# Two layers in fp32 pairs: a longer attention pipeline, low parts moved to POOL, a weight cast placed earlier, two plain up pages

## The chip, the cores and the metric

The kernel runs on one core of one Trainium2 chip. The metric is the device time of one execution in microseconds. Three runs of the kernel before took 2409.1, 2407.9 and 2407.92; their median is 2407.92.

## The reference

A block of 1024 tokens and 1024 features goes through two layers, all in float32. The first is a hybrid layer:

```python
h = rms_norm(x, norm_g)
u = jnp.einsum('bsd,dc->bsc', h, w_in)
v_c, b_c, c_c, z_c, q, k, v, z_a, gate_logits = jnp.split(u, SPLIT_POINTS, axis=-1)
y_c = b_c * causal_depthwise_conv(c_c * v_c, conv_w) * silu(z_c)
y_a = y_c @ w_conv_out
q, k = rms_norm(q), rms_norm(k)                       # 16 query heads, 4 key heads, 64 wide
o = sliding_window_attention(q, k, v, sinks) * silu(z_a)   # window 128, blocks of 128
y_b = o @ w_attn_out
g_a, g_b = split(sigmoid(gate_logits + gate_b))
x = x + (g_a * y_a + g_b * y_b) @ w_out
```

The second layer adds a mixer of pooled features and gated linear attention, a cross attention over 256 memory rows, and a feed-forward part: `u = h @ w_up` (2 x 2816 columns), a causal convolution of width three over each column of `u`, then `(silu(gate) * val) @ w_down`. A final rms norm ends it.

## The kernel before

**Number format.** Every large matrix product is done with float32 values cut in two: a high part (a cast to fp32r, on ScalarE) and a low part (value minus high part, one subtraction). A product is three matmuls, high by high, high by low, low by high. In the code names end in `h` and `l`, or `hi` and `lo`. Activations are kept transposed, feature by token, as tiles of 128 features by 512 tokens, in two halves `h`.

**Weights.** Weights arrive as pages of 128 x 1024 (512 KB): all of an output block's 1024 input rows. `Weights` walks a fixed list (`_stream`). `load` starts a DMA on SP into one of two raw buffers `wr`; `pf` casts the high part `wh` on ScalarE (two buffers) and puts the low part on a list `late`; `flush` (line 342) does the listed subtractions on VectorE, into `wl` (two buffers). `get` hands out a page and prefetches the next one. With `spare=True` the two parts go to other tiles, `wsh` and `wsl`.

**Plain and Strassen products.** A plain page is two calls of `dense` (line 381), one a half, each of 8 x 3 = 24 matmuls of 512 columns. Where two pages share an activation, `wino` (line 400) does both with seven products of 4 x 3 matmuls (a Winograd form of Strassen's scheme). It needs sums of the four quarters of the activation, T1 to T4, and of the two pages, S1 to S4. `sums` (line 448) makes the T on VectorE, with casts on ScalarE; `make` (line 290) makes the S on POOL (lines 298 to 306), with casts on ScalarE and low parts on VectorE (lines 302, 314, 330), one step a tick.

**Order of work.** All engines execute in the order in which the program is written; nothing reorders it. Side work is written as Python generators on the list `side`. `tick` flushes the low parts, moves `make` one step and moves every generator one step. `dense` ticks once in its middle and its caller once behind it, so that a plain page has four ticks. Tiles of PSUM: three banks `mm`, two `s`, two `t`, one `o`.

**The z pages.** At the start x goes through the norm in two halves. `first_two` runs the pages z0 and z1 on half 0, then both on half 1, whose tiles a side thread is still making; another side thread, `hT_sums`, makes T1 to T4 beside it, with quarters that it reloads from DRAM (`ht`, `hraw`). The third page is cast where `first_two` calls `W.pf()`, behind the product of z0 on half 1. Then come z2, z3 and the first pairs in `wino`.

**Attention.** While the pages `co` (conv output) and then `ao` (attention output) are multiplied, 16 halves each, the side generator `attention` (line 1160) runs 32 units, each of 4 heads over a block of 128 queries. In step i it does: the exponentials of unit i-1 on ScalarE (`expo`); the product with V of unit i-4 (`values`) into the single bank `o`, multiplied by VectorE into the head tiles (line 1155); for every second unit the difference of two blocks of V on POOL (`differ`); the scaling of unit i-1's probabilities by one over their sum on POOL (`finish`, line 1108); the transposes of unit i-2 on TensorE with their cut into high and low, and masked copies of both on POOL (`turn`, lines 1128 to 1138); the scores of unit i (`scores`, line 1078), copied by ScalarE and masked by VectorE, with row maxima. When a group of heads is done for a half, the four head tiles are cut one a step (`split`, low part on VectorE, line 377). At the start of half 1 of `co` the program waits for conv rows that another side thread (`reload`) is still bringing, with ticks that have no matmuls of their own.

**The up projection.** 22 pairs of pages (gate `fg`, value `fv`). The first FF_STD = 3 pairs run plain, the first in `first_two`, beside the norm of half 1 and the T sums; the rest run in `wino`. Behind each product stand its copy, three taps of the convolution (ScalarE, then two on VectorE, lines 1767 and 1768) and the gating (line 1775).

Of the kernel before, what the change touches and what calls it, by code (L numbers as in the profile page):

```python
# [11 lines left out]
ALU = mybir.AluOpType  # L12
# [8 lines left out]
DFF = 2816  # L21
NFF = DFF // P
FF_GROUPS = ((0, 6), (6, 12), (12, 18), (18, 22))
FF_STD = 3
POOL_WINDOWS = (2, 4, 8, 16)


# [51 lines left out]
def _stream():  # L79
    st = [("v", 0), ("v", 1)]  # L80
    st += [("z", 0, j) for j in range(4)]
    st += [("pair", ("z", 1, j), ("z", 1, j + 1)) for j in (0, 2)]
    st += [("pair", ("q", p, j), ("q", p, j + 1)) for p in range(2) for j in (0, 2)]
    st += [("pair", ("gb", m), ("gb", m + 1)) for m in range(0, KT, 2)]
    for c in range(KT):
        st += [("pair", ("cc", c), ("cv", c)), ("pair", ("cz", c), ("cb", c))]
    st += [("pair", ("ga", m), ("ga", m + 1)) for m in range(0, KT, 2)]
    st += [("co", m) for m in range(KT)] * 2
    st += [("ao", m) for m in range(KT)] * 2
    st += [("wo", m) for m in range(KT)] * 2  # L90
    st += [("p2", 0)]
    for p in range(2):
        st += [("q2", p), ("k2", p), ("v2", p, 0), ("v2", p, 1)]
    st += [("r2", 0), ("r2", 1), ("p2", 1), ("p2", 2), ("r2", 2), ("p2", 3), ("r2", 3)]
    st += [("wo2", m) for m in range(KT)] * 2
    for m in range(KT):
        st += [("xq", m), ("mk", m), ("mv", m // 4, m % 4)]
    st += [("xq", m) for m in range(KT)]
    st += [("xo", m) for m in range(KT)] * 2
    for f in range(NFF):  # L100
        st += [("fg", f), ("fv", f)] if f < FF_STD else [("pair", ("fg", f), ("fv", f))]
    for g in range(len(FF_GROUPS)):
        st += [("fd", g, m) for m in range(KT)]
    return st
# [12 lines left out]
def _body(es, tc, nc, wp, vec, xT, memT, gk2, pw, cst, out, dbg):  # L117
# [9 lines left out]
    V, S, G, T = nc.vector, nc.scalar, nc.gpsimd, nc.tensor  # L127
# [6 lines left out]
    def hp(s, dt=F32, shape=(P, HT)):  # L134
        return hpool.tile(list(shape), dt, name=nm(s), tag="hp")

    def tp(s, dt=F32, shape=(P, HT)):
        return tpool.tile(list(shape), dt, name=nm(s), tag="tp")
# [25 lines left out]
    def ps(tag, shape=(P, HT)):  # L164
        return psum.tile(list(shape), F32, name=nm("ps" + tag), tag=tag,
                         bufs={"mm": 3, "s": 2, "t": 2, "o": 1}[tag])

    def f(ap):
        return ap.bitcast(F32)
# [8 lines left out]
    def tick():  # L178
        W.flush()
        W.step()  # L180
        for g in list(side):
            if next(g, StopIteration) is StopIteration:
                side.remove(g)
# [23 lines left out]
    class Page:  # L207
        def __init__(self, his, los):
            self.his, self.los, self.n = his, los, 1024 // len(his)
# [19 lines left out]
    class Weights:  # L229
        def __init__(self):  # L230
            self.names = _stream()
            self.raw, self.cut = {}, {}
            self.late = []
            self.gen = None
            self.nd = self.ns = self.ng = self.out = 0
            self.limit = -1

        def load(self, name):
            n = ncols(name)
            raw = wpool.tile([P, 1024], F32, name=nm("wr"), tag="wr")  # L240
            nc.sync.dma_start(raw[:, :n], wp[PAGE[name], :, :n])
            self.out += 1
            return raw
# [98 lines left out]
        def flush(self):  # L342

            for lo, raw, hi in self.late:
                V.tensor_tensor(lo, raw, f(hi), ALU.subtract)  # L345
            self.late = []

        def get(self, name, pf=True, deep=False):
# [17 lines left out]
    W = Weights()  # L366
# [7 lines left out]
    def split(src, s, lo_in=None, eng=V):  # L374
        hi, lo = hp(s + "h", F32R), (lo_in or hp)(s + "l", F32R)
        S.copy(hi, src)
        eng.tensor_tensor(lo, src, f(hi), ALU.subtract)
        return hi, lo

    def mm3(out_ap, lh, ll, rh, rl, first, last):  # L380
        T.matmul(out_ap, lh, rh, start=first, stop=False)  # L381
        T.matmul(out_ap, lh, rl, start=False, stop=False)  # L382
        T.matmul(out_ap, ll, rh, start=False, stop=last)  # L383

    def dense(w, act, h, n=HT, msz=P, mid=None):

        o = ps("mm", (P, n))
        k = len(act)
        for kt in range(k):
            ah, al = act[kt][h]  # L390
            mm3(o[:msz], *w(kt * msz, msz), ah, al, kt == 0, kt == k - 1)
            if kt == k // 2 - 1:
                tick()
                if mid is not None:
                    mid()
        return o
# [115 lines left out]
            evac(dense(w, act, h), h)  # L512
            tick()

    def first_two(na, nb, act, ea, eb, spare=False):

        a = W.get(na)
        ea(dense(a, act, 0), 0)
        tick()
        b = W.get(nb, pf=False)  # L520
        eb(dense(b, act, 0), 0)
        tick()
        while None in [x[1] for x in act]:
            tick()
        if spare:
            W.pf(spare=True)
        o = dense(a, act, 1)
        if not spare:
            W.pf()
        ea(o, 1)  # L530
        tick()
        eb(dense(b, act, 1), 1)
        tick()
# [101 lines left out]
    def grid(n):  # L635
        return [[None, None] for _ in range(n)]
# [31 lines left out]
    hR, hT = grid(KT), grid(KT)  # L668
# [191 lines left out]
    def z_out(p, j, h, o):  # L860
        t = tp("z")
        S.activation(t, o, AF.Silu)
        zd[p, j, h] = dram("zd")
        nc.sync.dma_start(zd[p, j, h], t)
# [44 lines left out]
        wino((na, nb), X, lambda x: evac(0, 0, x), c22, c12, lambda y: evac(1, 0, y))  # L909

    side.append(hT_sums())
    first_two(("z", 0, 0), ("z", 0, 1), hT, *[lambda o, h, j=j: z_out(0, j, h, o) for j in range(2)])
    for j in (2, 3):
        both(("z", 0, j), hT, lambda o, h: z_out(0, j, h, o))
    while "T1" not in XB:
# [103 lines left out]
    qT, oT = {}, [[[None, None] for _ in range(4)] for _ in range(2)]  # L1019
# [137 lines left out]
    osp = grid(KT)  # L1157

    def attention():
        units = [Unit(p, h, b, half) for h in range(2) for p in range(2) for b in range(4) for half in range(2)]  # L1160
        n = len(units)
        todo = []
        dv = None
        for _ in range(5):
            yield
        for i in range(n + 4):
            if 0 <= i - 1 < n:
                units[i - 1].expo()
            if 0 <= i - 4 < n:
                units[i - 4].values(dv)  # L1170
                if i % 8 == 3:
                    u = units[i - 4]
                    todo += [(u.p, j, u.h) for j in range(4)]
            if i % 2 and 0 <= i - 3 < n and units[i - 3].n:
                dv = units[i - 3].differ()
            if 0 <= i - 1 < n:
                units[i - 1].finish()
            if 0 <= i - 2 < n:
                units[i - 2].turn()
            if i < n:  # L1180
                units[i].scores()
            if i in (8, 16):
                side.append(att_in(i // 16, 1))
            if todo:
                p, j, h = todo.pop(0)
                osp[4 * p + j][h] = split(oT[p][j][h], "o")
            yield
        while todo:
            p, j, h = todo.pop(0)
            osp[4 * p + j][h] = split(oT[p][j][h], "o")  # L1190
            yield
# [21 lines left out]
    while None in [yc[c][0] for c in range(KT)]:  # L1213
        tick()
    side.append(attention())
    for h in range(2):
        for m in range(KT):
            w = W.get(("co", m))
            gate_in(gin, gad, m + 1, h)
            if h == 0 and m == 3:  # L1220
                side.append(reload([(ycd[c][1], yc[c], 1) for c in range(KT)], "yc", 1, 1))
            while None in [yc[c][h] for c in range(KT)]:
                tick()
            o = dense(w, yc, h)
            t = gin[m, h]
            V.tensor_tensor(t, t, o, ALU.mult)
            mcd[m][h] = dram("mcd")
            nc.sync.dma_start(mcd[m][h], t)
            tick()
# [3 lines left out]
    def ao_in(m, h):  # L1233
        gate_in(gbi, gbd, m, h)
        gate_in(cin, mcd, m, h)

    xs = grid(KT)
    ao_in(0, 0)
    for h in range(2):
        for m in range(KT):  # L1240
# [7 lines left out]
            o = dense(w, osp, h)  # L1248
# [146 lines left out]
    o = glow_dense(1)  # L1395
# [136 lines left out]
    act = [cat[i] for i in order]  # L1532
# [301 lines left out]
    first_two(("fg", 0), ("fv", 0), xn, up0.plain(0), up0.plain(1), True)  # L1834
    for ft in range(1, FF_STD):
        up = Up(ft)
# [6 lines left out]
    fill_banks(XF["B11"][0][0])  # L1843
    for ft in range(FF_STD, NFF):
        if ft == NFF - 1:
# [26 lines left out]
    act = group(0, 0)  # L1872
# [5 lines left out]
    for g in range(1, 3):  # L1878
        act = group(g)
# [25 lines left out]
    act = group(3)  # L1905
    for h, c in ((0, slice(0, HT)), (1, slice(0, 256)), (1, slice(256, HT))):
        n = c.stop - c.start
        last = c.start > 0
        nrm, sqs = Norm(), []
        for m in range(KT):  # L1910
# [6 lines left out]
            o = dense(pages[m], [[None] * h + [(x[h][0][:, c], x[h][1][:, c])] for x in act], h, n)  # L1917
# [145 lines left out]
```

## Time and profile before

| | |
|---|---|
| profiled execution | 2407.34 us, of which the span of the trace 2405.6 |
| TensorE (PE) busy | 2366.1 us, 98%, 11574 matmuls |
| VectorE (DVE) busy | 1487.5 us, 62%, 2317 instructions |
| ScalarE (ACT) busy | 1009.5 us, 42%, 1869 |
| POOL busy | 577.8 us, 24%, 554 |
| DMA | 264.97 MB, mean 110 GB/s |

A row of the timeline gives start and duration in us, the engine, the line of the kernel, the operation, the tile written and those read, the shapes, and in brackets the idle time of that engine before it with what ended it. TensorE's instructions are pipelined: a duration is longer than the distance to the next start, so the distance between two starts is the rate.

### The profile page before, as it was taken

What the parts mean: (1) busy time and instruction counts of PE and PEld (TensorE: products, weight loads), DVE (VectorE), ACT (ScalarE), POOL (GpSimd) and SP (SyncE); (2) the same over time, 40 slices, a digit from 0 to 9 for tenths busy, and PEclk for the clock granted to TensorE, in tenths of its full rate; (3) what the DMA queues carried; (4) which work ended last, traced back from release to release, by engine and by line L of the source; (5) the groups of instructions that cost most, each with busy time, mean ns of one, the idle gap of its engine ahead of it and who ended that gap; (6) DMA issues with size and microseconds to landing.
All of it is one profiled execution on the core that took longest, in us unless ns stands there. A gap on an engine that the chain in (4) does not pass through costs nothing.

```text
span 2405.6 us, 30929 instructions
## 1 busy us (share of the span) xinstructions
PE 2366.1 (98%) x11574; PEld 1952.4 (81%) x11574; DVE 1487.5 (62%) x2317; ACT 1009.5 (42%) x1869; POOL 577.8 (24%) x554
## 2 busy tenths in 40 slices
PE   8999999999999999999999999999999999999998
PEld 8788888888887787887888888888888888888887
DVE  7744346666537997555445556455798888873435
ACT  5444433333346664334322334443555555552112
POOL 3235433333303552121001120001233333310003
PEclk9999999999999999999999999999999999999999
DMA  4533322122247534621100245322422222245222
GB/s 166 181 126 135 124 84 71 62 70 70 84 170 260 184 135 150 210 90 50 39 28 29 88 127 179 97 83 91 160 88 79 79 84 79 93 139 167 84 78 93
DMA packets 107510, 264.97 MB, mean 110 GB/s; under 512 B 12096, under 2 KB 14560, under 8 KB 107360
## 3 DMA queue, kind: packets, MB, share of 16 engines
q1 hardware_dynamic: 104880, 256.70, 31.3%
q0 software_dynamic: 1936, 5.77, 0.7%
q8 instruction: 91, 1.49, 0.2%
q10 hardware_dynamic: 544, 0.52, 0.1%
q14 instruction: 59, 0.48, 0.1%
HBM read 203.18 MB, written 59.77 MB: 109 GB/s over the span
## 4 chain that ended last, share of the span: by engine, by line
PE 88%; DVE 6%; ACT 3%; DMA 1%; issue 1%; POOL 0%; SPq 0%; DVEq 0%; POOLq 0%; ACTq 0%
PE psmm L381 14%; PE psmm L383 13%; PE psmm L382 13%; PE pss L410 6%; PE pss L412 5%; PE pss L411 5%; PE psmm L410 4%; PE psmm L412 4%; PE psmm L411 4%; PE pst L410 2%; PE pst L412 2%; PE pst L411 2%; PE pso L410 2%; PE pso L412 2%; PE pso L411 2%
## 5 line engine op out<-in xcount | busy, mean ns | idle before, releaser
L345 DVE TENSOR_TENSOR wl<-wr,wh 128x1024 fp32r<-128x1024 f32 (+1 forms) x147 | 180.3, 1226 | 97.7 <-ACT wh L281 97.5
L410 PE MATMUL pss<-T,wsh 128*128 128x512 f32 x588 | 232.0, 395 | 0.1
L412 PE MATMUL pss<-T,wsl 128*128 128x512 f32 x588 | 230.1, 391 | 0.0
L411 PE MATMUL pss<-T,wsh 128*128 128x512 f32 x588 | 229.4, 390 | 0.0
L330 DVE TENSOR_TENSOR wsl<-ws,wsh 128x512 fp32r<-128x512 f32 x196 | 208.3, 1103 | 33.4 <-ACT wsh L312 32.4
L564 POOL TENSOR_TENSOR sq<-sq,sq 128x512 f32<-128x512 f32 (+1 forms) x58 | 70.9, 1222 | 608.7 <-ACT sq L560 605.1
L281 ACT CAST wh<-wr 128x1024 fp32r<-128x1024 f32 (+1 forms) x147 | 148.2, 1008 | 149.7 <-PE psmm L382 128.5
L298 POOL TENSOR_TENSOR ws<-wr 128x512 f32<-128x512 f32 x49 | 69.8, 1425 | 567.5 <-DMA wr<-in_wp_dram 459.0
L381 PE MATMUL psmm<-xnh,wh 128*128 128x512 f32 x448 | 179.3, 400 | 5.0 <-ACT wh L281 5.0
L383 PE MATMUL psmm<-xnh,wl 128*128 128x512 f32 x448 | 175.9, 393 | 0.7 <-DVE wl L345 0.7
L382 PE MATMUL psmm<-xnl,wh 128*128 128x512 f32 x448 | 175.5, 392 | 0.0
L410 PE MATMUL psmm<-xnh,wh 128*128 128x512 f32 x392 | 153.9, 393 | 0.0
L412 PE MATMUL psmm<-xnh,wl 128*128 128x512 f32 x392 | 153.2, 391 | 0.0
L411 PE MATMUL psmm<-xnl,wh 128*128 128x512 f32 x392 | 152.6, 389 | 0.0
L410 PEld LDWEIGHTS pss<-T,wsh 128*128 128x128 f32 x588 | 110.4, 188 | 25.6 <-DVE cb L990 2.4
L412 PEld LDWEIGHTS pss<-T,wsl 128*128 128x128 f32 x588 | 110.3, 188 | 25.2
L411 PEld LDWEIGHTS pss<-T,wsh 128*128 128x128 f32 x588 | 110.4, 188 | 23.6
L383 PE MATMUL psmm<-fh,wl 128*128 128x512 f32 (+1 forms) x300 | 116.0, 387 | 1.1 <-DVE wl L345 1.1
L560 ACT ACTIVATE sq<-x 128x512 f32<-128x512 f32 (+1 forms) x80 | 47.1, 588 | 164.7 <-DVE x L1267 110.4
L381 PE MATMUL psmm<-fh,wh 128*128 128x512 f32 (+1 forms) x300 | 115.9, 386 | 0.0
L382 PE MATMUL psmm<-fl,wh 128*128 128x512 f32 (+1 forms) x300 | 115.9, 386 | 0.0
L302 DVE TENSOR_TENSOR wl<-wr,wh 128x1024 fp32r<-128x1024 f32 x49 | 66.0, 1346 | 70.8 <-ACT wh L296 70.8
(453 smaller groups left out, 6231.7 us busy)
## 6 DMA issues: line engine op xcount, KB each, us to landing
wr<-in_wp_dram SPq DMA_DIRECT2D x238, 512.0 KB, 3.7
act<-fa SPq DMA_DIRECT2D x44, 256.0 KB, 2.1
fr<-act SPq DMA_DIRECT2D x44, 256.0 KB, 4.4
wr<-in_wp_dram SPq DMA_DIRECT2D x24, 384.0 KB, 3.1
xd<-x SPq DMA_DIRECT2D x32, 256.0 KB, 4.4
x<-xd SPq DMA_DIRECT2D x32, 256.0 KB, 4.0
x<-in_xT_dram SPq DMA_DIRECT2D x16, 256.0 KB, 5.2
zd<-z SPq DMA_DIRECT2D x16, 256.0 KB, 2.0
```

Source lines behind the costliest of these rows:

```text
L281: S.copy(hi[:, :n], raw[:, :n])
L298: G.tensor_tensor(sg[0], a21, a22, ALU.add)
L302: V.tensor_tensor(l12, r1, f(h12), ALU.subtract)
L330: V.tensor_tensor(lo, raw, f(hi), ALU.subtract)
L345: V.tensor_tensor(lo, raw, f(hi), ALU.subtract)
L381: T.matmul(out_ap, lh, rh, start=first, stop=False)
L382: T.matmul(out_ap, lh, rl, start=False, stop=False)
L383: T.matmul(out_ap, ll, rh, start=False, stop=last)
L410: T.matmul(o, lh, rh, start=first and kt == 0, stop=False, skip_group_check=True)
L411: T.matmul(o, lh, rl, start=False, stop=False, skip_group_check=True)
L412: T.matmul(o, ll, rh, start=False, stop=kt == 3, skip_group_check=True)
L564: eng.tensor_tensor(self.acc, self.acc, sq, ALU.add)
```

## The change

Five edits. (1) In `attention` the step does the transposes of unit i-3 instead of i-2, the product of unit i-5 instead of i-4, and the difference of V for that unit, one step later each; the loop has 37 steps instead of 36. (2) The low part of a finished head tile is done on POOL inside that loop (those left over behind it stay on VectorE). (3) From the start of the attention to the end of the `co` pages, `flush` does the weights' low parts on POOL. (4) For the z pages `first_two` prefetches the third page right behind fetching the second, ahead of the second's product on half 0. (5) FF_STD is 2: the third up pair runs in `wino`.

```diff
-FF_STD = 3
+FF_STD = 2
...
             for lo, raw, hi in self.late:
-                V.tensor_tensor(lo, raw, f(hi), ALU.subtract)
+                self.eng.tensor_tensor(lo, raw, f(hi), ALU.subtract)
...
-    def first_two(na, nb, act, ea, eb, spare=False):
+    def first_two(na, nb, act, ea, eb, spare=False, ahead=False):
...
         b = W.get(nb, pf=False)
+        if ahead:
+            W.pf()
         eb(dense(b, act, 0), 0)
...
         o = dense(a, act, 1)
-        if not spare:
+        if not spare and not ahead:
             W.pf()
...
-        for i in range(n + 4):
+        for i in range(n + 5):
             if 0 <= i - 1 < n:
                 units[i - 1].expo()
-            if 0 <= i - 4 < n:
-                units[i - 4].values(dv)
-                if i % 8 == 3:
-                    u = units[i - 4]
+            if 0 <= i - 5 < n:
+                units[i - 5].values(dv)
+                if i % 8 == 4:
+                    u = units[i - 5]
                     todo += [(u.p, j, u.h) for j in range(4)]
-            if i % 2 and 0 <= i - 3 < n and units[i - 3].n:
-                dv = units[i - 3].differ()
+            if i % 2 == 0 and 0 <= i - 4 < n and units[i - 4].n:
+                dv = units[i - 4].differ()
             if 0 <= i - 1 < n:
                 units[i - 1].finish()
-            if 0 <= i - 2 < n:
-                units[i - 2].turn()
+            if 0 <= i - 3 < n:
+                units[i - 3].turn()
...
-                osp[4 * p + j][h] = split(oT[p][j][h], "o")
+                osp[4 * p + j][h] = split(oT[p][j][h], "o", eng=G)
...
     side.append(attention())
+    W.eng = G
     for h in range(2):
         for m in range(KT):
             w = W.get(("co", m))
...
     xs = grid(KT)
+    W.eng = V
     ao_in(0, 0)
```

## Rows read from the trace of the kernel before

**Rows 1.** The chain that ended last, its shares of the span by engine.
```profile
PE 88%; DVE 6%; ACT 3%; DMA 1%; issue 1%; POOL 0%; SPq 0%; DVEq 0%; POOLq 0%; ACTq 0%
```

**Rows 2.** Waits of TensorE, whole span: total us, times, longest us.
```profile
PE pso L1151 <- DVE o L1155: 6.7, 7, 1.9
...
PE pst L1128 <- POOL pr L1108: 2.3, 3, 1.2
```

**Rows 3.** Windows: length; busy us (instructions) of PE, PEld, DVE, ACT, POOL; clock; DMA.
```profile
722.00:760.00 38.00, 35.71 (x216) 27.32 (x214) 26.07 (x68) 21.14 (x65) 10.19 (x13) 1.00 0.85 318
760.00:800.00 40.00, 34.82 (x188) 26.44 (x187) 37.63 (x104) 28.21 (x93) 16.01 (x24) 0.87 0.56 192
800.00:870.00 70.00, 70.00 (x419) 56.31 (x418) 64.29 (x177) 47.54 (x162) 41.08 (x62) 1.00 0.48 164
870.00:930.00 60.00, 55.61 (x300) 43.27 (x299) 50.69 (x132) 35.15 (x113) 31.75 (x47) 0.97 0.27 93
...
92.36:99.17 6.81, 5.22 (x11) 3.64 (x12) 2.92 (x4) 4.96 (x8) 0.00 (x0) 0.50 0.55 185
```

**Rows 4.** Timeline of the z pages: ScalarE, TensorE and VectorE between 80 and 120 us.
```profile
81.67 0.60 ACT L862 ACTIVATE z<-psmm 128x512 f32<-128x512 f32 x1
92.81 1.04 ACT L281 CAST wh<-wr 128x1024 fp32r<-128x1024 f32 x1
...
93.91 0.79 PE L381 MATMUL psmm<-xnh,wh 128*128 128x512 f32 x1 [4.96 <-ACT wh L281]
119.58 0.39 PE L412 MATMUL psmm<-xnh,wl 128*128 128x512 f32 x1
...
100.02 0.69 DVE L482 TENSOR_TENSOR ht<-ht,x 128x512 f32<-128x512 f32 x1 [4.30 <-DMA ht<-hraw]
102.43 1.22 DVE L345 TENSOR_TENSOR wl<-wr,wh 128x1024 fp32r<-128x1024 f32 x1
115.84 1.21 DVE L302 TENSOR_TENSOR wl<-wr,wh 128x1024 fp32r<-128x1024 f32 x1
```

**Rows 5.** Groups of VectorE, 800 to 870: busy us, mean ns, idle before.
```profile
L345 DVE TENSOR_TENSOR wl<-wr,wh 128x1024 fp32r<-128x1024 f32 x5 | 7.4, 1484 | 0.0
L377 DVE TENSOR_TENSOR ol<-o,oh 128x512 fp32r<-128x512 f32 x7 | 5.9, 840 | 0.0
```

**Rows 6.** Groups of POOL, whole span: busy us, mean ns, idle before.
```profile
L305 POOL TENSOR_TENSOR ws<-wr,wr 128x512 f32<-128x512 f32 x49 | 82.2, 1677 | 0.0
...
L564 POOL TENSOR_TENSOR sq<-sq,sq 128x512 f32<-128x512 f32 (+1 forms) x58 | 70.9, 1222 | 608.7 <-ACT sq L560 605.1 <-issue 2.6 <-DVE sq L564 0.9
```

**Rows 7.** Timeline of TensorE: products of values at a bare tick, and steady.
```profile
787.30 0.47 PE L1151 MATMUL pso<-pch,vh 128*128 128x512 f32 x1 [2.54 <-ACT pr L1100]
...
805.88 0.40 PE L1151 MATMUL pso<-pch,vh 128*128 128x512 f32 x1
806.12 0.39 PE L1151 MATMUL pso<-pch,vl 128*128 128x512 f32 x1
...
811.56 0.40 PE L1151 MATMUL pso<-pch,vh 128*128 128x512 f32 x1
```

**Rows 8.** Timeline of ScalarE: the first exponential of two successive bare ticks.
```profile
785.08 0.20 ACT L1095 ACTIVATE sd<-sd 128x4 f32<-128x4 f32 x1 [3.25 <-DVE sd L1091]
...
790.42 0.20 ACT L1095 ACTIVATE sd<-sd 128x4 f32<-128x4 f32 x1 [0.76 <-DVE sd L1091]
```

**Rows 9.** Windows of the up stage, columns as in rows 3.
```profile
1753.90:1761.20 7.30, 7.30 (x34) 6.05 (x33) 6.90 (x13) 6.33 (x10) 0.00 (x0) 1.00 0.10 36
1773.80:1781.20 7.40, 7.40 (x34) 6.11 (x34) 7.03 (x6) 4.83 (x8) 7.27 (x4) 1.00 0.00 0
```

**Rows 10.** Timeline of the up stage: VectorE, SP's queue, TensorE's first fill matmuls.
```profile
1758.83 1.23 DVE L345 TENSOR_TENSOR wl<-wr,wh 128x1024 fp32r<-128x1024 f32 x1 [0.37 <-ACT wh L281]
...
1750.09 0.33 SPq L241 DMA_DIRECT2D wr<-in_wp_dram  x1
...
1783.59 0.62 PE L444 MATMUL pss<-xnh 128*128 128x512 f32 x2
```

More of the change, by code (lines that the diff above doesn't have):

```diff
@@ L236, in __init__ @@
             self.limit = -1
+            self.eng = V
         def load(self, name):
@@ L911, in _body @@
     side.append(hT_sums())
-    first_two(("z", 0, 0), ("z", 0, 1), hT, *[lambda o, h, j=j: z_out(0, j, h, o) for j in range(2)])
+    first_two(("z", 0, 0), ("z", 0, 1), hT, *[lambda o, h, j=j: z_out(0, j, h, o) for j in range(2)], ahead=True)
     for j in (2, 3):
```

## The prediction

> **What bounds the kernel now.** I began with the chain that ended last: 88% of the span runs over TensorE [rows 1]. It executes nearly the same matmuls after the change, so the question is where it stands still, and what takes over once it doesn't. The list of who waited for whom has VectorE's product out of the one-buffer PSUM tile `pso` as the longest wait, and POOL's scaling of the probabilities as a short one [rows 2]. The windows put both into the attention [rows 3]: TensorE is idle 2.3 us of 722–760, 5.2 of 760–800, none of 800–870, 4.4 of 870–930, together 11.9. After the longer stalls the granted clock falls to half (1.2 GHz): the mean of 0.87 in 760–800 and 0.97 in 870–930 is 0.13 x 40 + 0.03 x 60 = 7.0 us of lost clock, in part idle anyway. So the attention loses between 11.9 and 18.9 us; I take 17. VectorE is busy 37.6 of 40 us there and 64.3 of 70: it is what TensorE waits for.
>
> The second loss is at 89 us. TensorE stands for 5.0 us in front of the third z page, waiting for ScalarE's cast [rows 4], and then runs 6.8 us at half clock [rows 3], another 3.4: some 8 us. The up stage loses nothing: its windows have no idle time on TensorE, though VectorE is busy 6.9 of 7.3 us [rows 9].
>
> **Attention.** A steady tick, from one product of values to the next, is 5.68 us [rows 7]; a 512-column matmul takes 0.23 [rows 7], so the 12 of the dense half are 2.7 and the attention's own part is 3.0. Per tick VectorE has 64.3 x 5.68 / 70 = 5.2 us, POOL 41.1 x 5.68 / 70 = 3.3 [rows 3].
>
> The two moved kinds of work are 7.4 and 5.9 us of those 70 [rows 5], 1.1 us a tick: VectorE falls to 4.1. On POOL a 128x512 two-input operation has a mean of 1.22 us, or 1.68 for the group that meets most of VectorE's traffic [rows 6]. A page of weights has twice the columns and comes every second tick, so it adds 1.22 to 1.68 a tick; 13 of the 16 finished-head splits lie inside the loop of 37 steps, 0.43 to 0.59 a tick. POOL goes to 5.0, at most 5.6, of 5.68. I take the lower price, because the two-input SBUF operations that collide with POOL here are the very ones that leave VectorE; the row for the weights shows the collision now, 1.48 us against 1.23 elsewhere [rows 5, 10].
>
> The longer pipeline moves the transposes one tick later and the product of values one tick later. POOL's scaling then has 5.68 us more before TensorE asks for it; its waits (2.3 us) go [rows 2]. Behind a low part that POOL does late stands POOL's own queue (the differences of V, the scaling, the two masked copies), and TensorE is next to ask: for the differences one tick on, for the rest two. Finished low parts of weights are needed about a tick and a half after they are queued. Lags below some 5.7 us cost nothing.
>
> What stays: two ticks of the loop in `co` run without a dense half, since they only wait for the reloaded conv rows; at the first of them TensorE stands idle for 2.5 us [rows 7]. ScalarE and VectorE hand a loop to each other (exponentials, high part, score copies, masking, maximum, next exponentials) that takes 790.42 − 785.08 = 5.34 us [rows 8], and no part of the change shortens it. Two such ticks can cost 2 x (5.34 − 3.0) = 4.7; TensorE is now one product ahead, so I take 2.5. In the first `ao` pages the merge's cast stands in front of the exponentials on ScalarE and the low parts are back on VectorE: 1.5 left there. New loss 4, old 17: the attention gives **−13 us** (bounds: −17, and 0 if POOL's queue takes over).
>
> The Trainium skill (GPSIMD Engine Reference, Engine selection) speaks against this part: elementwise work with two inputs belongs on VectorE, POOL being about twice as slow. The trace agrees on the ratio (1.22 us for 512 columns against 1.23 for 1024). By that rule the move would be a loss; it is the fourth case below.
>
> **The cast ahead.** The z cast stood at 92.81 on ScalarE, behind a row of casts for the Strassen sums, which wait for VectorE [rows 4]. It now stands right behind the first z activation (81.67), done by about 84, its low part on VectorE by about 86; the wait at 88.9 is gone. It delays what stood between by 1.0 and 1.2 us, the same that is removed later. TensorE goes on at 88.8, needs the next page at about 100.1, and there it stops again: that page's low part runs at 102.43, because VectorE stands in order behind a sum whose input lands at 100.02 [rows 4]. That load is issued behind z's store, which moves by little. So TensorE waits from 100.5 to 103.8. It ends the page near 114.5 and meets the first pair's low part, 115.84 + 1.21 = 117.05, after the same chain of loads. Its third matmul stood at 119.58 [rows 4]; it can stand at 117.3, or at 118.9 if the clock falls again. Of 8 us lost, 2.3 or 0.7 come back: I take **−1.8** (bounds −8, 0).
>
> **Two plain up pages.** The third up pair was 8 x 12 = 96 matmuls and becomes 84: 12 x 0.23 = −2.7. Its price lies in VectorE's queue. The pair begins on TensorE at 1783.59 − 96 x 0.23 = 1761.5 [rows 10]. In the kernel before, the low part used there ran at 1758.83 and ended 1.4 us ahead of use [rows 10], though it is queued 36 matmuls ahead of it, at 1753.2: VectorE was over 5 us behind. Now the pair's first low part stands a tick later in that queue, behind two more sums and two conv taps (2.9 us); without more it would end near 1762.9, just in time. But POOL forms the pair's four weight sums as soon as the second page lands, about 3.8 us after 1750.09, in that very stretch. VectorE did 13 instructions in 7.30 us with POOL idle, and 6 in 7.40 us beside four such sums [rows 9]: some 3.5 us of its work are lost. The low part ends near 1766.2 against a use at 1762.7 (three fill matmuls and two others stand ahead): 3.5 us of wait, and 1.3 more for the low part of the pair's first sum. That is 4.8 − 2.7 = +2.1, and a little for the clock: **+2.5** (bounds −2.7 without a stall; +6 with one stretch of half clock as long as the one at 92 us).
>
> The Trainium skill (SBUF — State Buffer, SBUF: two separate sides) says that VectorE with two SBUF inputs and GpSimd lock one port pair against each other for whole instructions; the trace agrees, the 13 against 6 being its price.
>
> The attention's tiles don't hold the longer pipeline back: a score tile takes the buffer of a masked copy whose last product stands earlier in the same step, on TensorE ahead of the scores. The moved low parts free their raw buffers later by POOL's 1.2 us, against loads with a page of lead.
>
> **Sum.** −13 − 1.8 + 2.5 = −12.3. The profiled execution took 2407.3 (span 2405.6), so 2395.0; the median of the runs is 0.6 above it: **2395.6**.
>
> **Rivals.** *The up stage does not stall.* If VectorE catches up during the second plain page, the up stage gives −2.7: 2407.9 − 13 − 1.8 − 2.7 = 2390.4. For it: without POOL's sums the queue ends just in time. Against: what those sums cost VectorE in the next stretch [rows 9].
>
> *The ScalarE–VectorE loop is the attention's bound.* 5.34 us plus what stands between in order may be nearly the tick. Then only POOL's 2.3 us and some of the clock go, 5 in all: 2407.9 − 5 − 1.8 + 2.5 = 2403.6. For it: the loop crosses both engines every tick. Against: 800–870 has no idle TensorE though VectorE does 1.1 us a tick more there than it will.
>
> *POOL becomes the bound* (the slower side). In order, each tick of 3.3 us plus 1.36 times its price for 512 columns. At 2.2 us that is 6.3; over 36 ticks 0.62 x 36 = 22, less 5.7 of slack: the 17 us are back as waits for `wl` and for the transposes. From there it decides; at 2.3 us a piece the loss is 22, and the time 2407.9 + 5 + 0.7 = 2413.6. For it: 1.68 is a mean already. Against: that mean is taken beside VectorE's own two-input work.
>
> **Chances.** Forecast 0.58, no up stall 0.14, loop as bound 0.18, POOL as bound 0.10. What a measurement of this kernel can tell from no change is 0.2%, 4.8 us. The loop's case lies at that edge, 0.08 faster and 0.10 within; of POOL's, 0.04 is within and 0.06 slower. So faster 0.80, same 0.14, slower 0.06. The range goes from 2385 (the two first cases with z at its better end) to 2405 (past the loop's 2403.6); it leaves out POOL's case and the far ends.
>
> **What would show it.** Right: no wait of TensorE for POOL's scaling; clock 1.00 through 760–930 but near the two bare ticks; POOL over 80% busy in the co stage; the wait at 89 us gone and a shorter one for the next page's low part near 100; a wait for the low part of the up pair's first page where the sums of POOL run. Wrong: waits for `wl` on POOL, products of values still waiting for VectorE every few ticks, or an up pair that starts at once.

## The result, and the profile after

The changed kernel took 2442.11 us (median of 4 runs, 2441.41 to 2443.09) against 2408.51 for the kernel before on the same chip: ratio 1.0140, 95% interval 1.0122 to 1.0157, so 33.6 us slower where 12.3 faster was forecast. The profiled execution took 2441.41, its span 2439.7.

The chain of waits of the changed kernel, by engine (its row before is [rows 1]): TensorE's share fell from 88% to 81%, VectorE's and ScalarE's rose by 4 and 2 points, POOL's stayed at 0.
```profile
PE 81%; DVE 10%; ACT 5%; issue 2%; DMA 2%; POOL 0%; SPq 0%; DVEq 0%; POOLq 0%; ACTq 0%
```
TensorE's waits in the changed kernel between 700 and 1000 us (total, times, longest), which answer to [rows 2]: the wait for POOL's scaling is gone, as forecast; the one for VectorE's product out of `pso` went from 6.7 us to 18.6, and a new one, for VectorE's masking of the scores, stands beside it.
```profile
PE pso L1154 <- DVE o L1158: 18.6, 20, 3.5
PE pss L1081 <- DVE pr L1086: 10.4, 11, 2.6
```
Windows of the changed kernel, columns as in [rows 3]: in the steady stretch 800 to 870, where TensorE had no idle time, it is now idle for 7.4 us; over the four windows of [rows 3] its idle time went from 11.9 to 28.5. VectorE is less busy than before, though time in which an instruction of its own is held up counts as busy, and POOL is at 44.55 of 70: neither is full.
```profile
722.00:760.00 38.00, 32.28 (x185) 24.67 (x183) 21.86 (x56) 19.39 (x62) 14.86 (x10) 1.00 0.84 307
760.00:800.00 40.00, 32.36 (x176) 24.46 (x176) 35.64 (x87) 23.63 (x80) 25.39 (x33) 0.91 0.45 149
800.00:870.00 70.00, 62.63 (x352) 47.07 (x351) 56.93 (x142) 39.52 (x136) 44.55 (x55) 1.00 0.44 152
870.00:930.00 60.00, 52.27 (x284) 39.03 (x284) 49.39 (x117) 33.55 (x115) 39.31 (x51) 1.00 0.29 97
```
POOL's groups of the moved work in the changed kernel, 800 to 870 (busy us, mean ns, idle before), which answer to [rows 5]: the finished heads cost 1.29 us and a page 2.39, so 1.2 for 512 columns, as I had priced them.
```profile
L346 POOL TENSOR_TENSOR wl<-wr,wh 128x1024 fp32r<-128x1024 f32 x4 | 9.5, 2387 | 0.0
L378 POOL TENSOR_TENSOR ol<-o,oh 128x512 fp32r<-128x512 f32 x6 | 7.7, 1287 | 0.0
```
VectorE's small operations on the way from the row maximum to the exponentials are what grew: `mx` (the maximum times its scale), `nmx` (the negative maximum, clamped by the sink) and `sd` (the sink's own term), four columns each. First the row of the tile `nmx` in the kernel before, 722 to 990: duration in ns as min/median/max, then the first and last start; below it the same of the changed kernel.
```profile
L1089 DVE TENSOR_TENSOR nmx<-mx,nsink x32: 161/164/401, 732.6 to 913.6; 128x4 f32<-128x4 f32 x32
```
```profile
L1092 DVE TENSOR_TENSOR nmx<-mx,nsink x32: 161/766/2253, 730.9 to 940.4; 128x4 f32<-128x4 f32 x32
L1094 DVE TENSOR_TENSOR sd<-nmx,vt x32: 161/165/2310, 731.1 to 941.6; 128x4 f32<-128x4 f32 x32
```
Four columns take 0.16 us, and up to 2.3 in the changed kernel. The row also measures the loop: 32 units from the first `nmx` to the last took 181.0 us and take 209.5, 28.5 more. That is nearly the whole loss. One instance, in the timeline of the changed kernel on VectorE, POOL and ScalarE:
```profile
834.79 0.16 DVE L1090 TENSOR_TENSOR mx<-mx,rq 128x4 f32<-128x4 f32 x1
834.99 2.25 DVE L1092 TENSOR_TENSOR nmx<-mx,nsink 128x4 f32<-128x4 f32 x1
837.27 0.16 DVE L1094 TENSOR_TENSOR sd<-nmx,vt 128x4 f32<-128x4 f32 x1
...
834.21 0.64 POOL L1141 TENSOR_SCALAR_AFFINE_SELECT ppl<-pcl 128x512 fp32r<-128x512 f32 x1
834.81 2.40 POOL L346 TENSOR_TENSOR wl<-wr,wh 128x1024 fp32r<-128x1024 f32 x1
...
837.47 0.20 ACT L1098 ACTIVATE sd<-sd 128x4 f32<-128x4 f32 x1 [3.37 <-DVE sd L1094]
```
POOL starts a page's low part at 834.81; VectorE's `nmx`, issued 0.18 us later, ends at 837.24, 0.03 after POOL's instruction (834.81 + 2.40 = 837.21). ScalarE stands 3.37 us for it, and `nmx`, and with it the unit's exponentials, comes 2.1 us late. The masked copy that POOL runs at 834.21, with one input, ends 0.06 us after `mx` begins, so this instance can't tell whether it holds one up; experiment 4 can.

The z pages and the up stage went much as forecast. The changed kernel's timeline there, VectorE, TensorE and ScalarE of z, which answers to [rows 4]: the third page's cast stands at 83.32, its wait at 89 is gone; the next page's low part runs at 102.64 and the first pair's at 115.94, close to the times of the kernel before (102.43 and 115.84) that the prediction kept. TensorE waits 2.5 us for the first of them, up to 103.9, where 3.3 up to 103.8 were forecast.
```profile
102.64 1.22 DVE L346 TENSOR_TENSOR wl<-wr,wh 128x1024 fp32r<-128x1024 f32 x1
115.94 1.22 DVE L303 TENSOR_TENSOR wl<-wr,wh 128x1024 fp32r<-128x1024 f32 x1
...
103.91 0.77 PE L384 MATMUL psmm<-xnh,wl 128*128 128x512 f32 x1 [2.47 <-DVE wl L346]
...
83.32 1.05 ACT L282 CAST wh<-wr 128x1024 fp32r<-128x1024 f32 x1
```
Timeline of the up stage after, TensorE, POOL and VectorE, which answers to [rows 9, 10]: beside POOL's weight sums a VectorE operation takes 1.78 us where one took 0.68 just before, and TensorE waits 0.51 + 2.73 us in the pair that is no longer plain.
```profile
1793.10 0.50 PE L411 MATMUL psmm<-xnh,wh 128*128 128x512 f32 x1 [0.51 <-ACT wh L297]
1796.56 0.50 PE L413 MATMUL psmm<-xnh,wl 128*128 128x512 f32 x1 [2.73 <-DVE wl L303]
...
1783.62 1.38 POOL L299 TENSOR_TENSOR ws<-wr 128x512 f32<-128x512 f32 x1 [19.83 <-DMA wr<-in_wp_dram]
...
1783.17 0.68 DVE L479 TENSOR_TENSOR ft<-ft,ft 128x512 f32<-128x512 f32 x1
1783.77 1.78 DVE L1780 TENSOR_TENSOR fa<-fa,fa 128x512 f32<-128x512 f32 x1
1795.29 1.22 DVE L303 TENSOR_TENSOR wl<-wr,wh 128x1024 fp32r<-128x1024 f32 x1
```

### The profile page after: what moved, and what is told of

Its sections match the earlier page's. It is cut to its first block, busy times and chain, and to the rows that moved or that the text cites. A ratio compares the mean times of both kernels' runs of the same rounds, so it can differ in the third digit from the quotient of the medians.

```text
span 2439.7 us, 30930 instructions
## 1 busy us (share of the span) xinstructions
PE 2377.9 (97%) x11562; PEld 1955.1 (80%) x11562; DVE 1498.7 (61%) x2292; ACT 1011.2 (41%) x1874; POOL 632.7 (26%) x589
## 4 chain that ended last, share of the span: by engine, by line
PE 81%; DVE 10%; ACT 5%; issue 2%; DMA 2%; POOL 0%; SPq 0%; DVEq 0%; POOLq 0%; ACTq 0%
PE psmm L382 12%; PE psmm L384 12%; PE psmm L383 12%; PE pss L411 6%; PE pss L413 5%; PE pss L412 5%; PE psmm L411 4%; PE psmm L413 4%; PE psmm L412 4%; ACT pr L1103 2%; PE pst L411 2%; PE pst L413 2%; PE pst L412 2%; PE pso L411 2%; PE pso L413 2%; PE pso L412 2%
## 5 line engine op out<-in xcount | busy, mean ns | idle before, releaser
L411 PE MATMUL pss<-T,wsh 128*128 128x512 f32 x600 | 236.9, 395 | 0.5 <-DVE u L1805 0.4
L412 PE MATMUL pss<-T,wsh 128*128 128x512 f32 x600 | 234.0, 390 | 0.0
L346 DVE TENSOR_TENSOR wl<-wr,wh 128x1024 fp32r<-128x1024 f32 (+1 forms) x129 | 155.5, 1206 | 95.9 <-ACT wh L282 95.5
L282 ACT CAST wh<-wr 128x1024 fp32r<-128x1024 f32 (+2 forms) x145 | 146.1, 1008 | 147.9 <-PE psmm L383 127.9
L382 PE MATMUL psmm<-xnh,wh 128*128 128x512 f32 x416 | 166.5, 400 | 0.2 <-ACT z L865 0.2
L384 PE MATMUL psmm<-xnh,wl 128*128 128x512 f32 x416 | 163.5, 393 | 3.1 <-DVE wl L346 3.1
L383 PE MATMUL psmm<-xnl,wh 128*128 128x512 f32 x416 | 162.6, 391 | 0.0
L413 PE MATMUL psmm<-xnh,wl 128*128 128x512 f32 x400 | 157.2, 393 | 2.7 <-DVE wl L303 2.7
L411 PE MATMUL psmm<-xnh,wh 128*128 128x512 f32 x400 | 157.9, 395 | 0.5 <-ACT wh L297 0.5
L412 PE MATMUL psmm<-xnl,wh 128*128 128x512 f32 x400 | 156.4, 391 | 0.0
```

The source lines that it names most:

```text
L282: S.copy(hi[:, :n], raw[:, :n])
L346: self.eng.tensor_tensor(lo, raw, f(hi), ALU.subtract)
L411: T.matmul(o, lh, rh, start=first and kt == 0, stop=False, skip_group_check=True)
L412: T.matmul(o, lh, rl, start=False, stop=False, skip_group_check=True)
L413: T.matmul(o, ll, rh, start=False, stop=kt == 3, skip_group_check=True)
```

## The experiments

The theory that the trace suggests, "lock" (called "port" in the first expectations): while POOL runs an instruction with two SBUF inputs, a VectorE instruction with two SBUF inputs waits until it is over, however small it is. Rivals: the longer pipeline itself costs the time; POOL's own results come late (queue); any VectorE access suffers from POOL's traffic. All ratios are to the kernel before on the same chip in the same session, with 95% intervals; "loop" is the distance from the first to the last `nmx`, 181.0 us in the kernel before.

**1. The longer pipeline alone** (`pipe_only`).
```diff
-        for i in range(n + 4):
+        for i in range(n + 5):
...
-            if 0 <= i - 2 < n:
-                units[i - 2].turn()
+            if 0 <= i - 3 < n:
+                units[i - 3].turn()
```


> The kernel before with the longer attention pipeline alone; all low parts stay on VectorE, z cast and up pages as before. Theory (port): in the changed kernel a long two-input instruction of POOL holds a port that VectorE's four-column operations (row maximum times 1/rms, minimum with the sink) need, each waits for the whole of it, and these stand in the loop between ScalarE and VectorE; the pipeline is innocent: 2398 to 2407 us, the four-column minimum near 0.2 us. Rival (pipeline): the extra step itself holds tiles longer and makes the products wait: 2420 us or more. Rival (queue): POOL's own queue is late with low parts and scaling: as the theory here, 2398 to 2407.

Ratio 1.0002 (0.9993 to 1.0011), 2410.77 us: no change, above the 2398 to 2407 that the lock and the queue had in common. That clears the pipeline, and shows that the gain I expected of it did not come. TensorE's waits for POOL's scaling went, and VectorE's took their place; the waits of this kernel, 700 to 1000:
```profile
PE pso L1151 <- DVE o L1155: 8.8, 6, 3.0
PE pss L1078 <- DVE pr L1083: 2.7, 3, 1.1
```

**2. The low parts of the weights on POOL alone** (`w_low_only`).
```diff
+    W.eng = G
...
-                V.tensor_tensor(lo, raw, f(hi), ALU.subtract)
+                self.eng.tensor_tensor(lo, raw, f(hi), ALU.subtract)
```


> The kernel before with only the weights' low parts of the co pages on POOL. Port: most of the loss is here, 15 pages of about 2 us each in the loop less what VectorE gains: 2422 to 2436 us, the minimum again over 1 us on the mean. Rival (pipeline): VectorE is relieved, 2400 to 2408 us. Rival (queue): slower too, but with waits of TensorE for wl or for POOL's scaled probabilities in place of VectorE's products.

Ratio 1.0084 (1.0069 to 1.0099), +20.2 us: the largest part. The tile row of `nmx` in this kernel, and below it TensorE's waits for POOL: a loop of 202.2 us, 21.2 longer, and, with the short pipeline, 15 waits for POOL's scaling, which the full change hides.
```profile
L1090 DVE TENSOR_TENSOR nmx<-mx,nsink x32: 161/165/2326, 735.2 to 937.4; 128x4 f32<-128x4 f32 x32
```
```profile
PE pst L1129 <- POOL pr L1109: 7.3, 15, 1.8
```

**3. Pages in four pieces on POOL** (`pieces256`), the changed kernel with
```diff
-                self.eng.tensor_tensor(lo, raw, f(hi), ALU.subtract)
+                    for c in range(0, 1024, 256):
+                        c = slice(c, c + 256)
+                        G.tensor_tensor(lo[:, c], raw[:, c], f(hi[:, c]), ALU.subtract)
```


> The changed kernel with each page's low part on POOL in four instructions of 256 columns. Port: a small operation of VectorE waits for one piece, 0.6 us, not for 2.4: some 1.2 us back in each of 15 pages, 2418 to 2430 us. Rival (queue): the same work with more instructions on POOL, no gain: 2441 to 2450 us. Rival (pipeline): no change, 2442 us.

Ratio 1.0085 (1.0068 to 1.0102), some 13 us better than the changed kernel, at the low edge of the 12 to 24 that the lock had. A wait now ends with a piece; the longest `nmx` is as long as a finished head's low part (1.24):
```profile
L1097 DVE TENSOR_TENSOR nmx<-mx,nsink x32: 161/586/1237, 731.8 to 927.9; 128x4 f32<-128x4 f32 x32
```

**4. POOL held back until `sd` is done** (`gate`): a 4-column copy on POOL, read from `sd`, behind each unit's scores of the changed kernel.
```diff
+            G.tensor_copy(sm("gate", (P, 4)), sd)
             self.pr, self.nmx, self.sd = pr, nmx, sd
```


> The changed kernel with one more POOL instruction behind each unit's scores: a copy of the four-column value that VectorE makes last in the loop (sd). POOL executes in order, so the head's and the page's low part behind it start only when VectorE's small operations of that unit are done, that is beside the exponentials. Port: the waits of the small operations go, the attention loses little: 2400 to 2418 us. Rival (queue): POOL starts its long instructions later still: 2442 us or more. Rival (pipeline): 2442 us.

Ratio 1.0063 (1.0048 to 1.0078), 2425.96 us: 18.5 us better than the changed kernel, but past the 2418 at which the lock's range ended. No `nmx` is held any more (its tile row, first below); but ScalarE overwrites `sd` and so waits for the copy (ScalarE's waits, 700 to 1000, below it), which put POOL into the loop: 191.3 us.
```profile
L1092 DVE TENSOR_TENSOR nmx<-mx,nsink x32: 161/164/166, 730.9 to 922.2; 128x4 f32<-128x4 f32 x32
```
```profile
ACT sd L1099 <- POOL gate L1095: 62.6, 30, 3.6
```
The same trace answers what a POOL instruction with one SBUF input does. `mx` here begins while POOL's masked copy still has some 0.2 us to run, takes longer than its 0.16, and ends with it (833.61 + 0.21 against 833.17 + 0.64):
```profile
833.61 0.21 DVE L1090 TENSOR_TENSOR mx<-mx,rq 128x4 f32<-128x4 f32 x1
...
833.17 0.64 POOL L1142 TENSOR_SCALAR_AFFINE_SELECT ppl<-pcl 128x512 fp32r<-128x512 f32 x1
```
So do the eleven others of this trace that begin with over 0.15 us of it left, while those that begin later take their usual 0.16. The masked copy holds a two-input operation up too; the kernel before only meets it at its end.

**5 and 6. The same small operations with one SBUF input** (`one_input` on the changed kernel, `one_input_before` on the kernel before): one column at a time, the second factor as a per-partition scalar.
```diff
-            V.tensor_tensor(two(nmx), two(mx), self.sink(nsink), ALU.min)
+                V.tensor_scalar(nmx[:, e], mx[:, e], rqt[p, h][:, self.b, j, par:par + 1], nsink[:, k],
+                                op0=ALU.mult, op1=ALU.min)
...
-            V.tensor_tensor(den, den, self.sd, ALU.add)
+            for i in range(4):
+                V.tensor_scalar(den[:, i:i + 1], den[:, i:i + 1], self.sd[:, i:i + 1], None, op0=ALU.add)
```


> The changed kernel, with the four 4-column VectorE operations of a unit that read two SBUF tiles (maximum x scale, minimum with the sink, sd, sum of the denominators) written as 12 one-column operations that read one SBUF tile and take the other factor as a per-partition scalar. Same arithmetic. Lock theory (a two-input VectorE operation on SBUF waits for POOL's whole running instruction): these operations no longer wait, the means of nmx and sd fall from 1052 and 636 ns to under 200, although POOL's low parts keep their 2.4 us; the attention's stall falls from 49 us to 18 or less and the time to 2398-2415. Traffic rival (POOL's SBUF traffic slows every VectorE access): the one-column operations show means of several hundred ns too, time 2435-2450. Queue rival (TensorE and ScalarE wait for what POOL itself finishes late): nothing gets better, and the 8 additional operations a tick make it 2442-2455.

> The kernel before with the same rewrite of the small operations, as the control. If a one-column operation costs some 70 ns, 12 of them are 0.84 us against four of 160 to 270 ns (0.65 to 1.1): no change within 3 us, 2406-2412. If it costs 160 ns as the 4-column ones do, VectorE has up to 1.2 us a tick more and the time is 2415-2435. Lock theory beside it: POOL's two-input operations in the kernel before are 0.4 to 1.3 us long, so little of its stall is theirs, and the rewrite gains at most some 5 us.

The control missed my price: a one-column operation takes 210 to 267 ns, twelve of them 2.8 us a unit, and the rewrite alone costs 39 us (ratio 1.0164, 1.0150 to 1.0178). The changed kernel with it: 1.0148 (1.0134 to 1.0161). By its time alone the first run fits the queue's case; beside its control it doesn't. With two-input small operations the change costs 33.6 us, with one-input ones it costs nothing (0.0016 x 2409 = 3.9 less than its control, the two intervals overlapping). Not all of that difference need be the wait: the rewrite loads VectorE, so that its relief may be worth more, and it gives the control 13.4 us of waits for POOL's scaling, which the longer pipeline takes away. The tile rows and the timeline tell it without the times. The tile row of `nmx` in the rewritten changed kernel, and below it the timeline of VectorE and POOL in one of its units:
```profile
L1094 DVE TENSOR_SCALAR nmx<-mx,rq,nsink x128: 262/266/275, 730.8 to 943.4; 128x1 f32<-128x1 f32 x128
```
```profile
839.73 0.27 DVE L1094 TENSOR_SCALAR nmx<-mx,rq,nsink 128x1 f32<-128x1 f32 x1
...
839.33 2.39 POOL L346 TENSOR_TENSOR wl<-wr,wh 128x1024 fp32r<-128x1024 f32 x1
```
POOL's low part is as long as before, the operations beside it are not held, and none of 128 takes over 275 ns, though 82 of them begin while POOL is in a two-input operation. That excludes traffic as the cause, and ties the wait to the second SBUF tile that is read.

**7. The finished heads alone on POOL** (`heads_only`).
```diff
-                osp[4 * p + j][h] = split(oT[p][j][h], "o")
+                osp[4 * p + j][h] = split(oT[p][j][h], "o", eng=G)
```


> The kernel before with the low parts of the finished heads on POOL alone (13 operations of 1.3 us in the loop). Lock theory: in about half of 13 ticks a small operation of the loop waits up to 1.3 us: 3 to 8 us, 2412-2417, and the nmx mean rises over 273 ns in 800:870. Rival (VectorE's relief is worth something when the piece is short): 2403-2408. Rival (short pieces cost nothing either way, the loss of the changed kernel is all in the long pages): 2408-2410.

Ratio 1.0027 (1.0016 to 1.0038), +6.5 us; waits are as long as a head's low part, and the loop is 6.6 us longer:
```profile
L1089 DVE TENSOR_TENSOR nmx<-mx,nsink x32: 161/376/1223, 735.1 to 922.7; 128x4 f32<-128x4 f32 x32
```

**8. Three plain up pairs again** (`up3`, the changed kernel with `FF_STD = 3`).

> The changed kernel with the third up pair again as three plain pages (the last edit taken back). By the stall account of the changed kernel (6.6 us of stall in 1792 to 1815 against 2.7 saved): 2438, 3.9 less. Forecast of mine: 2439.6, 2.5 less. Rival (the stall would be hidden by later slack, the matmuls saved count): 2444.8, 2.7 more.

Ratio 1.0126 (1.0111 to 1.0142); the difference to the changed kernel is 3.4 us, between my forecast (2.5) and the account of its stalls (3.9). The two intervals overlap, so the times alone don't settle it, but the stall is seen to go. The window 1785 to 1820, first of the changed kernel, then of this one: no idle time is left.
```profile
1785.00:1820.00 35.00, 31.34 (x128) 24.43 (x127) 34.02 (x44) 21.06 (x36) 14.48 (x11) 0.95 0.25 83
```
```profile
1785.00:1820.00 35.00, 35.00 (x156) 28.99 (x155) 33.58 (x49) 22.68 (x36) 8.89 (x6) 1.00 0.26 91
```

**9. The cast ahead alone** (`ahead_only`).
```diff
+        if ahead:
+            W.pf()
         eb(dense(b, act, 0), 0)
```


> The kernel before with the z cast ahead alone. By the changed kernel's stalls in 50 to 150 us (5.2 us against 8.1): 2.9 us less than before, 2405-2408. My forecast for this edit: 1.8 less. Rival (what is gained at 89 us is given back at the first sums): 0, 2409-2411.

Ratio 0.9990 (0.9981 to 0.9999), 2406.07 us: 2.4 less, the only version here, with nothing left out, that beats both kernels, by half of what I had taken as the least that can be told; the interval just excludes no change. TensorE's waits in 50 to 150 of this kernel: 2.5 and 1.7 us, where the kernel before had one of 5.0 and the lower clock behind it.
```profile
PE psmm L383 <- DVE wl L345: 2.5, 1, 2.5
PE psmm L412 <- DVE wl L302: 1.7, 1, 1.7
```

**10 and 11. A gate that holds nobody else** (`gate2`, `gate2_heads`): pipeline, cast ahead and POOL's low parts, each behind a copy of `sd`, whose exponential goes to a tile of its own; in the second also the heads, in the other ticks.
```diff
+                if self.eng is G:
+                    behind()      # G.tensor_copy of the latest sd
                 self.eng.tensor_tensor(lo, raw, f(hi), ALU.subtract)
...
-            S.activation(self.sd, self.sd, AF.Exp)
+            es = sm("es", (P, 4))
+            S.activation(es, self.sd, AF.Exp)
```


> The kernel before with the longer pipeline, the cast ahead and the low parts of weights on POOL (finished heads stay on VectorE, third up pair plain), and each low part on POOL behind a 4-column copy of the latest sd, so that it begins when VectorE's small two-input operations of the tick are done; the exponential of sd goes to a tile of its own, so that ScalarE doesn't wait for that copy. Lock theory: nmx and sd at 160 to 200 ns, no loss left, and VectorE has 0.6 us a tick less: between 2396 (the relief is worth what I had forecast) and 2408 (it is worth nothing, and the cast ahead alone counts). Rival (POOL's low parts come too late or fill its queue, whatever locks): waits of TensorE for wl or for POOL's pr, 2412-2430.

> The same with the low parts of the finished heads on POOL as well, behind such a copy too and only in ticks whose slot has no low part of weights. Lock theory: as the run without the heads, 2394-2408, and at most as slow as that one. Rival (POOL has over 5 us a tick and becomes the bound): slower than that one by 3 us or more, with waits for POOL's pr.

`gate2`: 1.0004 (0.9995 to 1.0013), 2409.74, past the end of the range I gave the lock. Its loop is the old one again (181.4 us), since POOL's page now runs beside the exponentials; the tile row, then the timeline of one tick on VectorE and POOL (only `den`, the sum of the denominators, is held now, behind the exponentials):
```profile
L1100 DVE TENSOR_TENSOR nmx<-mx,nsink x32: 161/164/402, 731.0 to 912.4; 128x4 f32<-128x4 f32 x32
```
```profile
823.00 0.16 DVE L1102 TENSOR_TENSOR sd<-nmx,vt 128x4 f32<-128x4 f32 x1
825.35 0.45 DVE L1119 TENSOR_TENSOR den<-den,es 128x4 f32<-128x4 f32 x1 [1.29 <-ACT pr L1113]
...
823.23 0.19 POOL L375 COPY gate<-sd 128x4 f32<-128x4 f32 x1 [0.56 <-DVE sd L1102]
823.38 2.40 POOL L349 TENSOR_TENSOR wl<-wr,wh 128x1024 fp32r<-128x1024 f32 x1
```
So most of the loss of the low parts of weights is a matter of when POOL starts, not of what it costs: of 20.2 us some 3.7 are left, beside the cast ahead alone and with the pipeline's share in them. But nothing is gained. `gate2_heads` is 1.0020 (1.0011 to 1.0028), another 3.7 slower, which the lock had excluded and the rival had, though without the waits for POOL's scaling that the rival named; where its heads cost that is not settled.

**12. The moved work left out altogether** (`relief`): the longer pipeline, and in `co` and for the heads in the loop the high part stands in for the low part.
```diff
+                if self.names[self.ns][0] == "co":
+                    lo = hi
...
+        if eng is G:
+            return hi, hi
```


> The kernel before with the longer pipeline, and with the low parts that the change moves left out altogether: the co pages' and the 13 finished heads' products take the high part in the low part's place, so that TensorE does the same matmuls and neither VectorE nor POOL has that work. This is the most that moving it can give. The step of my forecast (VectorE's load is what TensorE waits for; 17 us of loss fall to 4): 2394-2399, with TensorE idle less than 4 us in 722 to 930. Rival (the stalls stand where the hand-over between ScalarE and VectorE sets the pace, at the two bare ticks and at the merges, whatever VectorE's load): 2403-2409, with the stalls near 733, 785, 792, 903 and 917 us still there.

Ratio 0.9978 (0.9969 to 0.9987), 2403.87 us, 5.3 less (7.5 to 3.1): the lower end of the rival's range. The loop took 174.2 us; of the five long stalls that the expectation lists, those near 792 and 903 are gone, the others stand, and over the four windows of [rows 3] TensorE is idle for 7.2 us, where it was 11.9 before and my step had under 4. Its tile row, TensorE's waits in 700 to 1000, and two windows as in [rows 3]:
```profile
L1095 DVE TENSOR_TENSOR nmx<-mx,nsink x32: 161/164/400, 734.3 to 908.5; 128x4 f32<-128x4 f32 x32
```
```profile
PE pso L1157 <- ACT pr L1106: 3.0, 1, 3.0
PE pso L1157 <- DVE o L1161: 2.4, 2, 2.2
PE pss L1084 <- DVE pr L1089: 1.8, 2, 1.1
```
```profile
760.00:800.00 40.00, 36.76 (x208) 28.66 (x205) 34.64 (x103) 27.88 (x93) 19.35 (x30) 0.91 0.56 196
870.00:930.00 60.00, 57.82 (x312) 46.14 (x311) 48.47 (x130) 35.17 (x109) 31.39 (x48) 1.00 0.29 99
```

## Why the prediction was wrong

**The sum.** Single edits against the kernel before: pipeline +0.5, weights +20.2, heads +6.5, cast ahead -2.4, plain up pages +3.4 (from `up3`), together +28.2. The whole change is +33.6. The other 5.4 stay open, and are no more than these intervals leave room for (4 us to either side for the whole change, 4 for the weights, 3 for the heads). Where POOL has a head and a page one after the other, `sd` is held as well, up to 2.31 us in the changed kernel and 0.39 at most with either edit alone; but that adds little to the loop, where 21.2 and 6.6 of the single edits already make 27.8 of the 28.5.

**The step that failed** is the attention's, "New loss 4, old 17", -13 us: the three edits there measure +32.6 (33.6 - 3.4 + 2.4). One of my signs of being wrong came: products of values that wait for VectorE, 20 of them. The step failed at two places.

First, at the price of POOL's work: "I take the lower price, because the two-input SBUF operations that collide with POOL here are the very ones that leave VectorE". The duration so taken was right (1.2 us for 512 columns), and POOL did not become the bound. But the large operations that leave are not the only ones with two SBUF inputs. Three of 4 columns stay, between the row maximum and the exponentials, in the very loop of 5.34 us of which I wrote that no part of the change shortens it, without asking what lengthens it. In [rows 5] the moved work was 13.3 us of 70; the changed kernel's VectorE stood for (1052 - 164) x 11 + (636 - 164) x 10 = 14.5 us in `nmx` and `sd` in the same window, by these groups (mean ns behind the busy us), and `mx` was held at times besides:
```profile
L1092 DVE TENSOR_TENSOR nmx<-mx,nsink 128x4 f32<-128x4 f32 x11 | 11.6, 1052 | 0.4
L1094 DVE TENSOR_TENSOR sd<-nmx,vt 128x4 f32<-128x4 f32 x10 | 6.4, 636 | 0.3
```
VectorE got back as waiting, inside the loop, what it had handed over from the loop's slack. The loss could be read in the trace of before: twelve of 32 `nmx` took 0.37 to 0.40 us there, beside POOL's short differences of V.

The Trainium skill (SBUF — State Buffer, SBUF: two separate sides) states the rule: the shared port pair goes to whichever starts first, for its whole instruction, and VectorE takes part with two SBUF inputs, against a POOL instruction that reads SBUF. The traces agree: four columns take 2.25 us beside a two-input operation of 2.40, and end with the masked copy, which has one input, where they meet it early enough (experiment 4). The prediction used that rule for the up stage, where it priced the first wait nearly right, and not for the attention.

Second, at the worth of relief. `relief` bounds it: with the moved work gone from both engines, and the longer pipeline, the gain is 5.3 us, not 13. My list of waits had VectorE's product as TensorE's longest wait and VectorE as busy 37.6 of 40 us; I read that as a matter of its load. The long stalls that remain in `relief` stand at a bare tick (one without matmuls of a page), where TensorE waits 3.0 us for ScalarE's exponentials themselves, and at a merge, 2.2 us, where VectorE's product stands in order behind a low part that waits for ScalarE's cast. The moved work was gone there and they stayed. The size is the one I gave to the rival that the ScalarE–VectorE loop is the bound ("5 in all"). Its argument against, that the steady stretch had no idle time, was true and spoke the other way: a stretch in which TensorE never waits has nothing to win from a lighter VectorE.

**What was right.** The pipeline removes the waits for POOL's scaling, as forecast, but the 2.3 us counted for them did not come back (+0.5, 2.2 to either side): VectorE's product was late behind them. The z stage: -2.4 against -1.8, with the new wait at the place forecast and 0.8 us shorter. Its loss before was a little oversized: of the 6.8 us at half clock TensorE had work in 5.2 [rows 3], so that they cost 2.6, not 3.4. The up stage: 3.4 against 2.5, with waits of 0.51 + 2.73 at the place named against 3.5; the 1.3 for the pair's first sum did not show as a wait, and the lower clock cost more than the little I gave it (0.05 x 35 = 1.8 us in the window of experiment 8), so that the sum agrees in part by luck. The rival in which POOL becomes the bound fell, and my sign that POOL would be over 80% busy did not come either: no wait for its low parts or its scaling, and 44.55 busy of 70.

## What to carry to other kernels

Before moving a two-input operation to POOL, list the two-input SBUF operations that stay on VectorE, the smallest too, and see which of them stand in a dependency loop: each can wait for a whole POOL instruction, and the price is POOL's duration, not theirs. Then the start time of POOL's work matters more than its amount: behind a short operation that waits for the loop's last such step, the low parts of the weights cost some 3.7 us here instead of 20.2. And bound the gain first: leave the work out and time it.

## What the runs showed of the hardware

A one-column VectorE operation with two per-partition scalars takes 266 ns, with one 210 to 214, so that four of them cost several times the 164 ns of one operation on four columns with a second SBUF tile. POOL's 128x1024 two-input subtraction takes 2.39 us, and 2.40 where VectorE waits for it: the engine that comes second pays. One SBUF input on POOL's side is enough: `mx`, begun 0.2 us before the end of POOL's masked copy, took up to 0.24 us in `gate` and ended with it. VectorE's product of values, which reads one SBUF tile and one in PSUM, is not held: four of them at 839.93 in `gate` took 0.98 us as elsewhere, although POOL's 128x1024 subtraction ran from 840.23 to 842.64.
